# Seeding the third PSUM bank of a Strassen block with a ScalarE copy of the first product

## The chip, the cores and the metric

The kernel runs on one core of a Trainium2 chip. The metric is the device time of one execution in microseconds (us). The engines are TensorE (PE in the profile, with PEld for its weight loads), VectorE (DVE), ScalarE (ACT), GpSimd (POOL) and SyncE (SP). PSUM, into which TensorE writes, has eight banks; the kernel keeps four of them for long sums and four for everything short.

## The reference

Two decoder layers over 256 tokens of width 1024, all in float32. Each layer is a mixer (retention in layer 0, block attention in layer 1) between two RMS norms, and then an MLP with a squared ReLU, whose hidden width is 4096:

```python
def sq_relu_mlp(x, w_up, w_down):
    h = jax.nn.relu(x @ w_up)
    return (h * h) @ w_down
...
for i in range(DEPTH):
    pre, post, w_in, w_out, mpre, mpost, w_up, w_down = layers[i]
    h = h + rms_norm(mixers[i % N_MIXERS](rms_norm(h, pre), w_in, w_out), post)
    h = h + rms_norm(sq_relu_mlp(rms_norm(h, mpre), w_up, w_down), mpost)
```

The change touches the product `x @ w_up` alone.

## The kernel before

**Splitting.** A float32 product is made of three fast matmuls. Every weight tile (128 x 1024, a chunk) is split by `Stream.split`: ScalarE writes the rounded high part `whi` (line 175), VectorE the rest `wlo` (line 176). The function `mm` then issues high x high (line 232), high x low (line 233) and low x high (line 234). The activations are split in the same way (lines 251 and 252). Chunks are prepared ahead of their use, in ten pairs of buffers.

**The MLP.** The 256 tokens are two blocks of 128 (t = 0, 1), and the hidden width is eight groups of 512. Groups 0 and 1 are computed plainly. The other six are done two at a time by `up_blocks(g, down)`, for g = 2, 4, 6, so there are three such blocks in each layer's MLP and six in the kernel; in this text they are blocks 1 to 6, the first three in layer 0. A block computes a 2 x 2 product by seven products of half the depth (Strassen's scheme in Winograd's form) instead of eight. Each product is twelve matmuls of 512 columns. They collect in three PSUM banks `x`, `y`, `z` (px, py, pz in the profile), and between them stands `down()`, which does one step of the second matmul of the MLP, `(h*h) @ w_down`, over both token blocks (tile dn).

**Sums in a block.** The first product goes to x, is copied to SBUF by ScalarE (p1, line 518), and x goes on collecting. y collects without it, and so wherever y is needed VectorE adds p1 from SBUF: for u2 (line 527), for u3 (line 531), and for the last quarter (line 463, called with `add=p1`). The next product into y has to wait until u2 has been read from it, since it overwrites what u2 is.

**Squares.** `squared` applies ReLU and square on ScalarE (lines 466, 467), waits some planned time, turns the tile by four TensorE transposes into a bank `tp_u` (line 256), and splits that into the hidden activations (lines 251 and 252). These hidden tiles are the operands of later `down()` steps.

**The order.** The order of instructions is written out when the program is built: `Flow` keeps a planned clock that moves on with every matmul, chains such as `squared` yield delays in it, and each engine then runs its instructions strictly in that order. Only semaphores decide the real times.

**The banks.** `new_ps` takes one of the four short banks that is free by the written order; it may be written only once all readers of its last tenant are done. In the last MLP (layer 1) one of the four is taken by `dn4` for the whole of it:

```python
acc = [[new_acc("dn") for _ in range(2)] for _ in range(NT)]
if nxt is None:
    acc[1] = [acc[1][0], acc[1][1][:, :256], new_ps([P, 256], "dn4")]
```

Of the kernel before, what the change touches and what calls it, by code (L numbers as in the profile page):

```python
# [13 lines left out]
AF = mybir.ActivationFunctionType  # L14
# [3 lines left out]
P = 128  # L18
# [198 lines left out]
def body(ctx, tc, xT, x, gT, gpost, w_in_0, w_out_0, w_up_0, w_down_0, w_in_1, w_out_1, w_up_1, w_down_1,  # L217
         cs0, dT, cs1, cmask, out):
    nc = tc.nc
# [17 lines left out]
    def mm_rows(o, a, w, s, first, last, again=False):  # L237

        mm(o, a, (w.hi[:, s], w.lo[:, s]), first, last, again)
        n = s.stop - s.start  # L240
        ws.used(w, n * P)
        flow.advance()
# [7 lines left out]
    def split(hi, lo, src):  # L250
        nc.scalar.activation(hi, src, AF.Copy)  # L251
        nc.vector.tensor_sub(lo, src, hi.bitcast(F32))  # L252

    def turn4(tp, src):
        for j in range(4):
            nc.tensor.transpose(out=tp[:, j, :], in_=src[:, j * P:(j + 1) * P], identity=ident)  # L256
        flow.now += 4 * P / 1200

    def new_act():
        return act.tile([P, 2048], F32R, tag="act", name="act")  # L260

    def new_acc(name):
        return psa.tile([P, 512], F32, tag="acc", name=name)

    def new_ps(shape, name):
        return psb.tile(shape, F32, tag="ps", name=name)

    def new_e2(shape, name):
        return work.tile(shape, F32, tag="e2", name=name, bufs=6)
# [4 lines left out]
    def small_t(tag, n=1):  # L274
        return small.tile([P, n], F32, tag=tag, name=tag)
# [53 lines left out]
    def load_gain(i):  # L329
        gb = work.tile([P, D], F32, tag="gb", name="gb", bufs=1)  # L330
        nc.sync.dma_start(gb, gpost[i:i + 1, :].to_broadcast([P, D]))
        return gb
# [58 lines left out]
    def step_out(acc, lhs, k, t, w, nk):  # L391
        a = lhs(k, t)
        c0 = 0
        for o in acc[t]:
            n = o.shape[-1]
            mm_rows(o, a, w, slice(c0, c0 + n), k == 0, k == nk - 1)
            c0 += n
# [32 lines left out]
    def in_groups_skewed(hT, then, ready=None):  # L430

        held = []
        hT.ready(0)
        for g in range(2):
            held.append([])
            o = new_acc("ip")
            for c in range(4):
                held[g].append(ws.get())
                in_tile(hT, held[g][c], c, 0, o)
            then(g, 0, o)  # L440
        hT.ready(1)
        if ready:
            ready()
        for g in range(2):
            o = new_acc("ip")
            for c in range(4):
                in_tile(hT, held[g][c], c, 1, o)
            then(g, 1, o)


    def mlp(hT, gain, nxt, gi, qpool):
        ws.open_quads([qpool.tile([P, 2, CH], F32, name=f"quad{i}") for i in range(4)])
        hid = [None] * NG
        done = [[] for _ in range(NG)]

        def new_hid(g):
            hid[g] = new_act().rearrange("p (u j s) -> p u j s", u=2, j=4)

        def squared(g, t, o, add=None, sign=1.0, delay=4.0):

            c = new_e2([P, 512], "c")
            if add is not None:
                nc.vector.tensor_add(c, o, add)
                yield 2.2
                o = c
            nc.scalar.activation(c, o, AF.Relu, scale=sign)
            nc.scalar.activation(c, c, AF.Square)
            yield delay
            tp = new_ps([P, 4, P], "tp_u")
            turn4(tp, c)  # L470
            ts = slice(t * P, (t + 1) * P)
            split(hid[g][:, 0, :, ts], hid[g][:, 1, :, ts], tp)

        def square(g, *args):
            done[g].append(flow.spawn(squared(g, *args)))

        s_hi, s_lo = [p.tile([P, 4, 4, P], F32R, name=n, tag="act" if p is act else n)
                      for p, n in ((act, "s_hi"), (qpool, "s_lo"))]

        def block_sums():  # L480

            (a11, a12), (a21, a22) = [[hg[:, t, e::2, :] for e in range(2)] for t in range(NT)]
            f = [new_e2([P, 4, P], "hsum") for _ in range(4)]
            nc.vector.tensor_sub(f[0], a22, a21)
            yield 1.5
            nc.vector.scalar_tensor_tensor(f[1], f[0], -1.0, a11, op0=ALU.mult, op1=ALU.subtract)
            split(s_hi[:, 0], s_lo[:, 0], f[0])
            yield 2.8
            nc.vector.tensor_sub(f[2], a11, a21)
            split(s_hi[:, 1], s_lo[:, 1], f[1])  # L490
            yield 2.8
            nc.vector.scalar_tensor_tensor(f[3], f[1], -1.0, a12, op0=ALU.mult, op1=ALU.subtract)
            split(s_hi[:, 2], s_lo[:, 2], f[2])
            yield 2.8
            split(s_hi[:, 3], s_lo[:, 3], f[3])

        def quad(t, e):
            return lambda kp: hT.tile(2 * kp + e, t)

        def hsum(i):  # L500
            return lambda kp: (s_hi[:, i, kp, :], s_lo[:, i, kp, :])

        def product(o, lhsT, first):

            for half in range(2):
                w = ws.get()
                for kk in range(2):
                    kp = 2 * half + kk
                    mm_rows(o, lhsT(kp), w, slice(kk * 512, (kk + 1) * 512), first and kp == 0, kp == 3,
                            not first)  # L510

        def up_blocks(g, down):


            x = new_ps([P, 512], "px")
            product(x, quad(0, 0), True)
            p1 = new_e2([P, 512], "p1")
            nc.scalar.activation(p1, x, AF.Copy)
            down()
            flow.finish(*sums)  # L520
            z = new_ps([P, 512], "pz")
            product(z, hsum(0), True)
            down()
            y = new_ps([P, 512], "py")
            product(y, hsum(1), True)
            u2 = new_e2([P, 512], "u2")
            nc.vector.tensor_add(u2, y, p1)
            down()
            product(y, hsum(2), False)
            u3 = new_e2([P, 512], "u3")  # L530
            nc.vector.tensor_add(u3, y, p1)
            square(g + 1, 1, z, u3, -1.0, 6.0)
            down()
            product(x, quad(0, 1), False)
            square(g, 0, x, None, 1.0, 6.5)
            down()
            product(y, quad(1, 1), False)
            square(g, 1, y, p1)
            down()
            product(z, hsum(3), False)  # L540
            square(g + 1, 0, z, u2, -1.0)
            down()
            down()

        def lhs(k, t):
            g, j = divmod(k, 4)
            flow.finish(*done[g])
            return hid[g][:, 0, j, t * P:(t + 1) * P], hid[g][:, 1, j, t * P:(t + 1) * P]

        new_hid(0)  # L550
        new_hid(1)
        sums = []
        in_groups_skewed(hT, lambda g, t, o: square(g, t, o, None, 1.0, 3.6),
                         lambda: sums.append(flow.spawn(block_sums(), 1.0)))
        gb = load_gain(gain)
        rs2 = []
        for t in range(NT):
            r2 = small_t("rs2")
            nc.gpsimd.tensor_tensor(r2, hT.rs[t], hT.rs[t], ALU.mult)
            rs2.append(r2)  # L560
# [3 lines that stand above are left out]
        nk = FF // P  # L564
        ks = iter(range(nk - SKEW))

        def down():
            k, w = next(ks), ws.get()
            for t in range(NT):
                step_out(acc, lhs, k, t, w, nk)  # L570

        for g in range(2, NG, 2):
            new_hid(g + 1)
            new_hid(g)
            up_blocks(g, down)
        ws.quads = None
        if nxt is not None:
            nxt = nxt()
            finish_out(acc, lhs, nk - SKEW, nk, rs2, gb, nxt, gi)
            return nxt  # L580
        finish_last(acc, lhs, nk, rs2, gb)
# [34 lines left out]
    hT = HT()  # L616
# [207 lines left out]
    hT = HT()  # L824
# [4 lines left out]
    with tc.tile_pool(name="qpool0", bufs=1) as qpool:  # L829
        hT = mlp(hT, 1, HT, 2, qpool)  # L830
# [170 lines left out]
    hT = HT()  # L1001
# [102 lines left out]
```

## Time and profile before

| | us |
|---|---|
| median of 3 runs (674.85 to 675.34) | 675.29 |
| the profiled execution, its own time | 675.31 |
| its span, first to last instruction | 673.5 |
| busy: PE | 663.2 (98%) |
| busy: DVE | 495.1 (74%) |
| busy: ACT | 409.3 (61%) |
| busy: POOL | 103.5 (15%) |

The busy time of PE is the union of pipelined matmuls. What one matmul takes of PE's time is therefore read from the distance between the starts of neighbours, and a wait from a distance that is longer than the others. Times in the rows are counted from the start of the span, and a row's line number is that of the kernel shown above; a helper's line is shared by all its callers, and the tile names tell them apart.

### The profile page before, as it was taken

To read this page: it belongs to the slowest core of one execution; us is meant where nothing else is said; L and a number is where in the kernel's file an instruction comes from. 1 tells how busy PE (TensorE), PEld (TensorE's weight loads), DVE (VectorE), ACT (ScalarE), POOL (GpSimd) and SP (SyncE) were. 2 spreads that over 40 slices of the span, in tenths; PEclk is the share of its full clock that TensorE was granted. 3 is DMA by queue.
4 is the path that set the end of the run, shared out by engine and by line. 5 is a ranking of instruction groups with operands and counts; after the bars stand their busy time and mean duration, and the time that the engine had idled before them with its cause. 6 is when DMAs were issued, how large, how long until landed. Compare 5 with 4: busy or idle time off the path is not lost.

```text
span 673.5 us, 9114 instructions
## 1 busy us (share of the span) xinstructions
PE 663.2 (98%) x3371; PEld 559.3 (83%) x3371; DVE 495.1 (74%) x595; ACT 409.3 (61%) x575; POOL 103.5 (15%) x162
## 2 busy tenths in 40 slices
PE   8999999999999999999999999999999999999996
PEld 6888898988888888888888888888888888888885
DVE  5579675674547998878975876776669998788733
ACT  6555644544536777856774766766567668566731
POOL 0024120111000111101100161914001111011001
PEclk9999999999999999999999999999999999999999
DMA  7867655446629489696648557544284997956511
GB/s 278 319 207 250 204 188 198 163 157 211 205 87 384 112 263 332 153 377 159 187 144 264 173 176 228 168 148 157 76 361 97 307 300 167 375 129 188 176 44 62
DMA packets 38924, 137.61 MB, mean 204 GB/s; under 512 B 4576, under 2 KB 4832, under 8 KB 38880
## 3 DMA queue, kind: packets, MB, share of 16 engines
q1 hardware_dynamic: 35280, 124.44, 52.2%
q0 software_dynamic: 3456, 12.58, 10.6%
q8 instruction: 26, 0.43, 0.3%
q14 instruction: 18, 0.15, 0.1%
q10 hardware_dynamic: 144, 0.02, 0.0%
HBM read 123.39 MB, written 1.05 MB: 185 GB/s over the span
## 4 chain that ended last, share of the span: by engine, by line
PE 91%; DMA 3%; issue 2%; DVE 1%; ACT 1%; POOL 1%; SPq 0%; POOLq 0%; DVEq 0%; ACTq 0%
PE ip L232 9%; PE ip L233 9%; PE ip L234 9%; PE dn L234 8%; PE dn L232 8%; PE dn L233 8%; PE out L234 3%; PE out L232 3%; PE out L233 3%; DMA raw<-in_w_in 3%; PE py L232 3%; PE py L234 2%; PE py L233 2%; PE tp_u L256 2%; PE px L232 2%
## 5 line engine op out<-in xcount | busy, mean ns | idle before, releaser
L176 DVE TENSOR_TENSOR wlo<-raw,whi 128x1024 fp32r<-128x1024 f32 (+1 forms) x179 | 214.8, 1220 | 57.6 <-ACT whi L175 56.7
L175 ACT ACTIVATE whi<-raw 128x1024 fp32r<-128x1024 f32 (+1 forms) x179 | 180.6, 1037 | 24.6 <-PE out L234 10.9
L232 PE MATMUL ip<-whi,act 128*128 128x512 f32 x288 | 114.2, 396 | 0.4 <-DVE csr L708 0.4
L233 PE MATMUL ip<-wlo,act 128*128 128x512 f32 x288 | 112.4, 390 | 0.0
L234 PE MATMUL ip<-whi,act 128*128 128x512 f32 x288 | 112.4, 390 | 0.0
L176 DVE TENSOR_TENSOR wlo<-quad,whi 128x1024 fp32r<-128x1024 f32 x84 | 101.1, 1222 | 13.0 <-ACT whi L175 12.7
L232 PE MATMUL dn<-whi,act 128*128 128x512 f32 (+1 forms) x288 | 106.8, 371 | 0.0
L234 PE MATMUL dn<-whi,act 128*128 128x512 f32 (+1 forms) x288 | 105.7, 367 | 0.0
L233 PE MATMUL dn<-wlo,act 128*128 128x512 f32 (+1 forms) x288 | 105.3, 366 | 0.0
L175 ACT ACTIVATE whi<-quad 128x1024 fp32r<-128x1024 f32 x84 | 86.6, 1050 | 22.6 <-DMA quad<-quad 17.2
L234 PEld LDWEIGHTS ip<-whi,act 128*128 128x128 f32 x288 | 54.1, 188 | 11.6
L232 PEld LDWEIGHTS ip<-whi,act 128*128 128x128 f32 x288 | 54.2, 188 | 11.0 <-issue 0.8
L233 PEld LDWEIGHTS ip<-wlo,act 128*128 128x128 f32 x288 | 54.2, 188 | 10.1
L234 PEld LDWEIGHTS dn<-whi,act 128*128 128x128 f32 x288 | 54.2, 188 | 9.8 <-DVE act L252 0.9
L233 PEld LDWEIGHTS dn<-wlo,act 128*128 128x128 f32 x288 | 54.3, 188 | 9.1
L232 PEld LDWEIGHTS dn<-whi,act 128*128 128x128 f32 x288 | 54.2, 188 | 9.0
L185 POOL DMA_DIRECT2D quad<-quad x24 | 21.1, 881 | 190.4 <-DMA raw<-in_w_down 75.2
L232 PE MATMUL out<-whi,act 128*128 128x512 f32 x96 | 37.8, 394 | 0.0
L234 PE MATMUL out<-whi,act 128*128 128x512 f32 x96 | 37.4, 390 | 0.0
L251 ACT ACTIVATE act<-tp_u 128x512 fp32r<-128x512 f32 x32 | 19.1, 596 | 30.1 <-PE tp_u L256 30.1
L233 PE MATMUL out<-wlo,act 128*128 128x512 f32 x96 | 37.4, 389 | 0.0
L232 PE MATMUL qk<-act,whi 128*128 128x256 f32 x128 | 36.7, 287 | 0.5 <-ACT whi L175 0.5
(187 smaller groups left out, 1098.6 us busy)
## 6 DMA issues: line engine op xcount, KB each, us to landing
raw<-in_w_in SPq DMA_DIRECT2D x72, 512.0 KB, 4.4
raw<-in_w_down SPq DMA_DIRECT2D x64, 512.0 KB, 5.5
quad<-in_w_up SPq DMA_DIRECT2D x48, 512.0 KB, 7.6
raw<-in_w_out SPq DMA_DIRECT2D x24, 512.0 KB, 4.1
quad<-quad POOLq DMA_DIRECT2D x24, 512.0 KB, 5.9
raw<-in_w_up SPq DMA_DIRECT2D x16, 512.0 KB, 3.4
gb<-in_gpost SPq DMA_DIRECT2D x4, 512.0 KB, 6.3
h<-in_x SPq DMA_DIRECT2D x2, 512.0 KB, 6.7
```

The lines of the kernel that those rows point to most:

```text
L175: nc.scalar.activation(hi[:, c], raw[:, c], AF.Copy)
L176: nc.vector.tensor_sub(lo[:, c], raw[:, c], hi[:, c].bitcast(F32))
L185: nc.gpsimd.dma_start(o, a, accum_op=ALU.add)
L232: nc.tensor.matmul(o, a[0], b[0], start=first, stop=False, skip_group_check=again)
L233: nc.tensor.matmul(o, a[0], b[1], start=False, stop=False, skip_group_check=again)
L234: nc.tensor.matmul(o, a[1], b[0], start=False, stop=last, skip_group_check=again)
L251: nc.scalar.activation(hi, src, AF.Copy)
L256: nc.tensor.transpose(out=tp[:, j, :], in_=src[:, j * P:(j + 1) * P], identity=ident)
```

## The change

```diff
             x = new_ps([P, 512], "px")
             product(x, quad(0, 0), True)
-            p1 = new_e2([P, 512], "p1")
-            nc.scalar.activation(p1, x, AF.Copy)
             down()
             flow.finish(*sums)
+            y = new_ps([P, 512], "py")
+            nc.tensor.matmul(y, hT.tile(0, 0)[0], s_hi[:, 0].rearrange("p k s -> p (k s)"), start=True, stop=True)
+            nc.scalar.activation(y, x, AF.Copy)
             z = new_ps([P, 512], "pz")
             product(z, hsum(0), True)
             down()
-            y = new_ps([P, 512], "py")
-            product(y, hsum(1), True)
+            product(y, hsum(1), False)
             u2 = new_e2([P, 512], "u2")
-            nc.vector.tensor_add(u2, y, p1)
+            nc.scalar.activation(u2, y, AF.Copy)
             down()
             product(y, hsum(2), False)
             u3 = new_e2([P, 512], "u3")
-            nc.vector.tensor_add(u3, y, p1)
+            nc.scalar.activation(u3, y, AF.Copy)
             square(g + 1, 1, z, u3, -1.0, 6.0)
             down()
             product(x, quad(0, 1), False)
             square(g, 0, x, None, 1.0, 6.5)
             down()
             product(y, quad(1, 1), False)
-            square(g, 1, y, p1)
+            square(g, 1, y)
```

The bank y is taken before z now. One matmul (line 522 of the changed kernel) writes 512 columns into it, with values that nobody reads, so that the bank counts as written; ScalarE then overwrites it with the first product (line 523), and all products into y add to that. u2 and u3 become plain ScalarE copies of y (lines 529 and 533), and the ReLU of the last quarter reads y itself.

TensorE in block 4 (the first of layer 1), from the transposes of the last plain square to the first product into z. Before (numbers are buffers; what stands in brackets is the engine whose semaphore is waited for):

```order
L256 MATMUL tp_u_4996<-ident_100,c_4947 128x128 [waits PE_49,Activation_49]
...
L234 MATMUL dn4_4960<-whi_4881,act_4722 128x256
L232 MATMUL pz_5022<-whi_4900,s_hi_4720 128x512 [waits PE_49]
L233 MATMUL pz_5022<-wlo_4901,s_hi_4720 128x512
...
L232 MATMUL py_5066<-whi_4972,s_hi_4720 128x512 [waits DVE_49]
```

The same place in the changed kernel:

```order
L256 MATMUL tp_u_4991<-ident_100,c_4944 128x128 [waits PE_49,Activation_49]
...
L234 MATMUL dn4_4957<-whi_4878,act_4719 128x256
L522 MATMUL py_5017<-s_hi_4717,act_4468 128x512 [waits PE_49]
L232 MATMUL pz_5020<-whi_4897,s_hi_4717 128x512 [waits DVE_49]
L233 MATMUL pz_5020<-wlo_4898,s_hi_4717 128x512
...
L232 MATMUL py_5017<-whi_4969,s_hi_4717 128x512 [waits Activation_49]
```

The wait for VectorE has moved from the first product into y to the first product into z, 21 matmuls of 512 columns and 6 of 256 earlier; in the built programs the bank of tp_u goes to py before the change and to pz after it.

VectorE in block 4 up to the read of that tp_u, in the changed kernel; before the change the same instructions stand there in the same order, only with other numbers:

```order
L252 TENSOR_TENSOR act_4719<-tp_u_4925,act_4719 128x4x128 [waits Activation_49]
L176 TENSOR_TENSOR wlo_4939<-raw_4742,whi_4938 128x1024 [waits DMAHW1_49,Activation_49]
L252 TENSOR_TENSOR s_lo_4718<-hsum_4845,s_hi_4717 128x512 [waits Activation_49]
L176 TENSOR_TENSOR wlo_4970<-quad0_4713,whi_4969 128x1024 [waits Activation_49]
L176 TENSOR_TENSOR wlo_4981<-quad0_4713,whi_4980 128x1024 [waits Activation_49]
L252 TENSOR_TENSOR act_4720<-tp_u_4991,act_4720 128x4x128 [waits Activation_49]
```

Nothing has moved here: the read of tp_u stays behind five others.

ScalarE in block 1, around the new copies u2 and u3, in the changed kernel:

```order
L175 ACTIVATE whi_2378<-quad3_2031 128x1024
L529 ACTIVATE u2_2388<-py_2328 128x512
L175 ACTIVATE whi_2393<-raw_2197 128x1024
L175 ACTIVATE whi_2405<-quad0_2028 128x1024
L175 ACTIVATE whi_2418<-quad0_2028 128x1024
L533 ACTIVATE u3_2428<-py_2328 128x512
L175 ACTIVATE whi_2435<-raw_2257 128x1024
```

Before the change the five splits (line 175) stand there without the two copies; the copies now stand between splits that are prepared for later products.

## Rows read from the trace of the kernel before

**Rows 1.** The page: span, engine busy times, granted TensorE clock in 40 slices.

```profile
span 673.5 us, 9114 instructions
PE 663.2 (98%) x3371; PEld 559.3 (83%) x3371; DVE 495.1 (74%) x595; ACT 409.3 (61%) x575; POOL 103.5 (15%) x162
...
PEclk9999999999999999999999999999999999999999
```

**Rows 2.** Waits of PE: who waited for whom, total us, times, longest us.

```profile
PE warm L283 <- DVE junk L278: 1.2, 1, 1.2
...
PE qk L234 <- DVE wlo L176: 0.4, 2, 0.2
```

**Rows 3.** Timeline of PE in block 1, product into z and its successor: start us, us.

```profile
236.55 0.39 PE L232 MATMUL pz<-whi,s_hi 128*128 128x512 f32 x1
...
239.28 0.39 PE L232 MATMUL dn<-whi,act 128*128 128x512 f32 x1
```

**Rows 4.** Timeline of PE in block 1, at the second product into y.

```profile
247.21 0.39 PE L234 MATMUL dn<-whi,act 128*128 128x512 f32 x1
247.62 0.47 PE L232 MATMUL py<-whi,s_hi 128*128 128x512 f32 x1
247.93 0.40 PE L233 MATMUL py<-wlo,s_hi 128*128 128x512 f32 x1
```

**Rows 5.** Timeline of PE in block 4, at the second product into y.

```profile
531.70 0.28 PE L234 MATMUL dn<-whi,act 128*128 128x256 f32 x1
531.88 0.47 PE L232 MATMUL py<-whi,s_hi 128*128 128x512 f32 x1
532.19 0.39 PE L233 MATMUL py<-wlo,s_hi 128*128 128x512 f32 x1
```

**Rows 6.** The tile py, columns: duration ns minimum/median/maximum, first and last start us.

```profile
L527 DVE TENSOR_TENSOR u<-py,p x6: 690/692/692, 246.8 to 615.7; 128x512 f32<-128x512 f32 x6
```

**Rows 7.** The tile px: same columns.

```profile
L518 ACT ACTIVATE p<-px x6: 577/580/582, 236.7 to 605.3; 128x512 f32<-128x512 f32 x6
```

**Rows 8.** Timeline of DVE in block 1 at the same place.

```profile
246.78 0.69 DVE L527 TENSOR_TENSOR u<-py,p 128x512 f32<-128x512 f32 x1
```

**Rows 9.** Timeline of ACT in block 1, around the place of u2; idle before, releaser.

```profile
241.47 1.99 ACT L175 ACTIVATE whi<-quad 128x1024 fp32r<-128x1024 f32 x2
243.37 1.04 ACT L175 ACTIVATE whi<-raw 128x1024 fp32r<-128x1024 f32 x1
246.10 1.06 ACT L175 ACTIVATE whi<-quad 128x1024 fp32r<-128x1024 f32 x1 [1.68 <-DMA quad<-quad]
```

**Rows 10.** Timeline in block 1: the last matmul of the first product into y.

```profile
244.49 0.39 PE L234 MATMUL py<-whi,s_lo 128*128 128x512 f32 x1
```

**Rows 11.** Timeline in block 1: the split behind u3 on DVE, its use on PE.

```profile
253.50 1.22 DVE L176 TENSOR_TENSOR wlo<-raw,whi 128x1024 fp32r<-128x1024 f32 x1
262.05 0.39 PE L233 MATMUL dn<-wlo,act 128*128 128x512 f32 x1
```

**Rows 12.** Timeline of DVE in block 1: the read of tp_u.

```profile
239.38 0.69 DVE L252 TENSOR_TENSOR act<-tp_u,act 128x512 fp32r<-128x512 f32 x1
```

**Rows 13.** Timeline of PE in block 4, from the transposes to the product into z.

```profile
518.70 0.60 PE L256 MATMUL tp_u<-ident,c 128*128 128x128 f32 x4
...
520.82 0.39 PE L232 MATMUL pz<-whi,s_hi 128*128 128x512 f32 x1
```

**Rows 14.** Timeline of DVE in block 4, at the same time.

```profile
519.03 0.69 DVE L252 TENSOR_TENSOR act<-tp_u,act 128x512 fp32r<-128x512 f32 x1
...
521.37 2.36 DVE L176 TENSOR_TENSOR wlo<-quad,whi 128x1024 fp32r<-128x1024 f32 x2
523.64 0.69 DVE L252 TENSOR_TENSOR act<-tp_u,act 128x512 fp32r<-128x512 f32 x1
```

**Rows 15.** Timeline in block 5: DVE's read of tp_u, PE's product into z.

```profile
563.35 0.69 DVE L252 TENSOR_TENSOR act<-tp_u,act 128x512 fp32r<-128x512 f32 x1
564.12 0.40 PE L232 MATMUL pz<-whi,s_hi 128*128 128x512 f32 x1
```

## The prediction

> **What bounds the kernel now.** I read the page's busy line first, then the waits of PE, then PE's timeline in the six blocks. PE is busy for 663.2 of 673.5 us and its granted clock is in the top tenth in all 40 slices, that is, 2.4 GHz [rows 1]. A high busy share alone would not say that PE sets the end, but the waits do: PE's list has five lines, the longest single wait is 1.2 us, at the start, and none of the five is in an MLP [rows 2]. In a block, the twelve 512-column matmuls of a product take 2.73 us from the first start to the start of what follows, 0.2275 each [rows 3]. So whatever is added to PE in a block is paid in full, and work taken from DVE (74%) or given to ACT (61%) [rows 1] moves the time only where PE waits for it. The question is therefore not what VectorE saves, but which waits of PE go and which come.
>
> **What the change adds to PE.** Six matmuls of 512 columns, one a block, in a stream that has no holes: 6 x 0.2275 = 1.37 us [rows 3]. From below this could be nothing for one that stands ahead of a wait; from above I take 0.31, the distance that a matmul right after a wait shows [rows 4, 5], so 6 x 0.31 = 1.86. I take 0.2275, since the matmul has the shape and type of its neighbours. The Trainium skill ("TensorE: Matmul & The Clock Gate", section "Back-to-back issue gap") puts a sustained stream of 512-column matmuls at about 131 ns each. This trace does not agree; by that figure, as an estimate, the six would be 0.79 us and the sum below 0.58 lower.
>
> **What it moves between ScalarE and VectorE.** VectorE loses three additions a block, 18 x 0.69 = 12.4 us [rows 6]. ScalarE keeps one copy (px into PSUM instead of SBUF) and gains two, 12 x 0.58 = 7.0 us [rows 7]. No row shows ScalarE writing PSUM: I take the 0.58 of the copy into SBUF, and even twice that ends long before the next product into y, which stands behind a product into z and a down step, 24 matmuls or 5.4 us [rows 3]. None of this is on PE's path by itself. Two effects are.
>
> First, a gain. The second product into y waits until u2 is read. In block 1 VectorE, which has a queue, reads it only at 246.78 to 247.47 [rows 8], and PE starts at 247.62: 0.41 after its neighbour instead of 0.23, and the matmul after it again 0.08 late, 0.27 in all [rows 4]. In block 4 it is 0.18 instead of the half of 0.23 for a 256-column neighbour, and again 0.08: 0.14 [rows 5]. The other four blocks show no such gap. On ScalarE, u2 stands behind two splits that end at 243.46 [rows 9], and y is ready at 244.88 [rows 10]: the copy ends near 245.7, some 1.5 us ahead of the old end, and before PE asks. So both gaps go: -0.41 us. The bound on the other side is that they stay: 0.
>
> Second, who is queued behind the two copies on ScalarE: splits of weights. The copies wait for PE there, so the split behind u2 starts some 2 us later than its 243.37 [rows 9]. That costs only if a weight comes late. The split behind u3 is finished by VectorE at 254.72 and used by PE at 262.05, 7.3 us later [rows 11]; VectorE, which does the second half of each split, has 0.69 less to do ahead of it. I cost this at nothing; it is paid from a delay of about 7 us on.
>
> The square of the last y quarter now skips one addition, so its transposes come some 2 us earlier on PE. There are as many as before, and ScalarE's ReLU and square have four planned us: nothing.
>
> **The bank.** This is the largest term, and the diff does not show it. y is taken before z, so at the start of the product into z four tiles must have a bank: x, y, z, and the last tp_u if it is still unread. In layer 0 there are four short banks, and it fits: in block 1 tp_u is read by VectorE only at 239.38, long after z began at 236.55, and nothing waits [rows 3, 12]. In layer 1 dn4 holds one of the four. In block 4 the tp_u of the last plain square is written at 518.70 and z begins at 520.82 [rows 13]; VectorE reads tp_u at 523.64 to 524.33, because two splits of 2.36 us together stand before it in its queue [rows 14]. Before the change y took that bank, one product and one down step later, and it was free by then. In the changed program y takes the last free bank and z takes that of tp_u, so the first matmul into z waits for VectorE, and the whole of PE behind it, in order. VectorE's queue up to there is the same as before and runs without gaps, so its end stays at 524.33. PE starts 0.15 us after such a release (247.47 to 247.62) [rows 4, 8], at 524.48, and would have been ready at 520.82 + 0.23 = 521.05: 3.43 us, and 0.08 for the matmul after the wait. Together 3.51 us. Nothing gives this back: behind it PE has no long waits in layer 1's MLP that could absorb it [rows 2].
>
> Blocks 5 and 6 have the same three banks. There VectorE's read ended at 564.04 and z began at 564.12 [rows 15]; the new z comes 0.23 later and waits for 0.15 after the read, so it would be on time by 0.16 even unchanged. VectorE has additions less ahead of it, so I cost this at nothing; as an upper bound, 0.3 us a block if the read slips.
>
> **The sum.** 675.31 (the profiled execution; its span is 673.5, and 1.8 lies around it) + 1.37 + 3.51 - 0.41 = 679.78. The profiled execution is 0.02 above the median 675.29, so no correction: **679.8 us**, 0.7% slower. Its own range: down to 678.9 (the wait 0.5 shorter, the matmul of block 4 and one more at nothing), up to 680.9 (+0.5 for matmuls at 0.31, +0.6 for blocks 5 and 6).
>
> **Rivals.**
>
> *The bank is free in time* (not slower). If VectorE's read of tp_u ended before about 520.9 in block 4, z would not wait, and the time is 675.31 + 1.37 - 0.41 = 676.3, within 0.2% of the median (that is, up to 676.6), which is about what a measurement of this kernel can tell from no change. For it: in the other five blocks the bank is in time. Against it: it needs 3.4 us on VectorE, whose order there has not moved and whose removed additions all come later. Chance 0.10.
>
> *The clock falls.* A gap of 3.4 us on PE is three times the longest in this trace [rows 2], and all stretches of it have 2.4 GHz [rows 1]; what PE does after so long a gap is not shown. If it went on at 1.2 GHz for the product into z, twelve matmuls would cost 12 x 0.2275 = 2.7 us more, 682.5. Against it: the 1.2 us gap at the start left no mark. The Trainium skill (same page, section "HAM oscillation — how this bites in real kernels") says that waits of TensorE can put its clock back to half. No row here shows it. Chance 0.10.
>
> *ScalarE's waits starve PE of weights.* From a delay of 7 us [rows 11], which would take several of the new waits in a row with the waits for DMA that stand there already (1.68 us at 246.10 [rows 9]). Priced at 2 us or more, 681.8 and up. Chance 0.03.
>
> *VectorE's relief pays more than the six matmuls cost.* This would have to come from waits of PE that I don't see. Chance 0.01.
>
> **How the numbers follow.** The forecast has 0.76, the free bank 0.10, the clock 0.10, starved weights 0.03, relief 0.01. The range is the forecast's own with the clock case, 678.9 to 682.5, which holds 0.86. Slower by over 0.2%: 0.76 + 0.10 + 0.03 = 0.89; the same: 0.10; faster: 0.01.
>
> **What would show it.** In the new trace: the extra matmul of each block 0.23 before the next start; a hole of some 3.4 us in PE in block 4 alone, at the first matmul into z, released by VectorE's read of tp_u (line 252); no gap at the second product into y in blocks 1 and 4; u2 and u3 on ScalarE near 0.58; blocks 2, 3, 5 and 6 longer by 0.23 each. No hole in block 4 makes the forecast wrong at its largest term; a hole with a granted clock below 9 tenths behind it is the clock rival.

## The result and the profile after

The changed kernel takes 681.07 us (median of 6 runs, 680.76 to 682.2), the kernel before on the same chip 675.4 (674.85 to 676.2): ratio 1.0082, 95% interval 1.0072 to 1.0093. It is slower by 5.7 us. The profiled execution took 681.0 us, its span is 679.2.

The page of the changed kernel, in the form of [rows 1]:

```profile
span 679.2 us, 9111 instructions
...
PE 666.3 (98%) x3377; PEld 561.6 (83%) x3377; DVE 485.0 (71%) x577; ACT 414.5 (61%) x587; POOL 105.6 (16%) x162
...
PEclk9999999999999999999999999999999999999999
```

VectorE's busy time fell by 10 us and ScalarE's rose by 5, and neither shows in the time. PE's busy time grew by 3.1 us for six matmuls of 0.23, which come to 1.4 only; the clock line, in tenths of a slice of 17 us, gives no reason. Both are answered only from nearer.

The waits of PE, as in [rows 2] (total us, times, longest):

```profile
PE pz L232 <- DVE act L252: 3.2, 1, 3.2
...
PE warm L283 <- DVE junk L278: 1.2, 1, 1.2
```

One line is new, and it is the longest: the first matmul of a product into z waits once for VectorE's splitting of tp_u. PE's timeline in block 4 (start us, us; in brackets idle before and releaser) shows it at the place of [rows 13]:

```profile
520.83 0.39 PE L522 MATMUL py<-s_hi,act 128*128 128x512 f32 x1
524.38 0.50 PE L232 MATMUL pz<-whi,s_hi 128*128 128x512 f32 x1 [3.17 <-DVE act L252]
524.73 0.40 PE L233 MATMUL pz<-wlo,s_hi 128*128 128x512 f32 x1
...
525.67 0.39 PE L234 MATMUL pz<-whi,s_lo 128*128 128x512 f32 x1
525.89 0.58 PE L232 MATMUL pz<-whi,s_hi 128*128 128x512 f32 x1
526.27 0.63 PE L233 MATMUL pz<-wlo,s_hi 128*128 128x512 f32 x1
...
529.26 0.44 PE L234 MATMUL dn<-whi,act 128*128 128x512 f32 x1
529.54 0.39 PE L232 MATMUL dn<-whi,act 128*128 128x512 f32 x1
```

From 520.83 to 524.38 are 3.55 us for one matmul of 0.23: a hole of 3.32, and the matmul behind it comes another 0.12 late. The next five run at the usual distance. From 525.89 on, the distance is mostly 0.43 instead of 0.23, up to 529.54: nine matmuls take 3.65 us, where 9 x 0.2275 = 2.05 would do. That is 1.60 us lost where PE is busy and waits for nothing. VectorE's timeline has the releaser at the same time as in [rows 14]:

```profile
523.65 0.68 DVE L252 TENSOR_TENSOR act<-tp_u,act 128x512 fp32r<-128x512 f32 x1
```

It ends at 524.33, and PE starts 0.05 later. The windows of the same stretch (window, length, busy us of PE, PEld, DVE, ACT, POOL with instructions, granted clock, DMA share, GB/s) name what made the nine matmuls slow:

```profile
520.83:524.38 3.55, 0.39 (x3) 0.07 (x1) 3.55 (x6) 3.55 (x6) 1.16 (x2) 1.00 0.72 265
524.38:526.27 1.89, 1.89 (x7) 1.52 (x8) 1.89 (x2) 1.89 (x3) 0.58 (x1) 0.91 1.12 247
526.27:529.50 3.23, 3.23 (x9) 2.57 (x8) 3.23 (x4) 1.48 (x2) 0.00 (x0) 0.52 1.00 192
529.50:534.00 4.50, 4.50 (x24) 3.79 (x23) 1.64 (x2) 0.00 (x0) 0.00 (x0) 1.00 1.04 317
```

The granted clock is 0.52 from 526.27 to 529.50, that is 1.2 GHz for nearly all of it, and 2.4 GHz again behind it. PE had stood idle for 3.3 us shortly before. The Trainium skill ("TensorE: Matmul & The Clock Gate", section "HAM oscillation — how this bites in real kernels") says that waits of TensorE can send its clock back to half; this trace agrees, with 0.52 behind the hole of 3.3 us.

How much of the 5.7 us is in this one place is read from the first matmul into x, at which a block starts. Block 4 of the changed kernel begins and ends at:

```profile
514.61 0.40 PE L232 MATMUL px<-whi,act 128*128 128x512 f32 x1
...
563.30 0.40 PE L232 MATMUL px<-whi,act 128*128 128x512 f32 x1
```

That is 48.69 us, where it was 43.52 before (514.60 to 558.12). The table gives four blocks of each kernel that is spoken of here, each from its first matmul into x to that of the next block, and the stretch from the start of block 1 to the start of the kernel's last matmul. This stretch leaves out the first 230 us, whose length differs by more than 1 us between profiles. The clock has a part in that too. In four of the twelve profiles here (changed with 4 in the hole; changed, y behind z; before, no dn4; changed, no seeding matmul) the granted clock is 0.50 from 10 to 12 us after the start, and block 1 starts at 231.31 to 231.63; in the eight others it stays at 1.00 there, and block 1 starts at 229.94 to 230.88. One of the four, with y behind z, has in the window from 10 to 20 us:

```profile
10.00:20.00 10.00, 10.00 (x75) 10.00 (x75) 8.42 (x12) 7.15 (x11) 0.00 (x0) 0.86 0.87 310
```

The kernel's first 230 us are the same work in all twelve. PE's longest wait between its first matmul and that stretch is 0.7 to 1.0 us in the four, and 0.2 to 1.4 in the others.

| kernel | block 1 | block 2 | block 4 | block 5 | block 1 to last matmul | less before |
|---|---|---|---|---|---|---|
| before | 43.33 | 42.73 | 43.52 | 43.18 | 436.60 | |
| changed | 43.22 | 42.96 | 48.69 | 43.42 | 442.54 | +5.94 |
| changed, 14 matmuls in the hole | 43.23 | 42.96 | 47.08 | 43.41 | 440.94 | +4.34 |
| changed, 4 in the hole | 43.21 | 42.96 | 47.07 | 43.41 | 440.92 | +4.32 |
| changed, 8 in the hole | 43.23 | 42.96 | 47.10 | 43.41 | 440.97 | +4.37 |
| before, bank taken in block 4 | 43.31 | 42.73 | 49.71 | 43.17 | 442.73 | +6.13 |
| changed, y behind z | 43.24 | 42.96 | 44.58 | 43.42 | 438.48 | +1.88 |
| before, no dn4 | 43.31 | 42.74 | 43.30 | 42.74 | 434.99 | -1.61 |
| changed, no dn4 | 43.24 | 42.96 | 43.27 | 42.97 | 435.82 | -0.78 |
| before, four more matmuls a block | 43.92 | 43.63 | 44.29 | 44.08 | 441.55 | +4.95 |
| changed, copies on VectorE | 43.26 | 42.96 | 49.76 | 43.42 | 443.68 | +7.08 |
| changed, no seeding matmul | 43.01 | 42.73 | 43.39 | 43.19 | 436.13 | -0.47 |

In the changed kernel blocks 2 and 5 are longer by 0.23 and 0.24, the one matmul each. Block 1 is shorter by 0.11: 0.23 more for the matmul, and some 0.3 less, since the gap of [rows 4] is gone:

```profile
247.13 0.39 PE L234 MATMUL dn<-whi,act 128*128 128x512 f32 x1
247.36 0.39 PE L232 MATMUL py<-whi,s_hi 128*128 128x512 f32 x1
247.59 0.39 PE L233 MATMUL py<-wlo,s_hi 128*128 128x512 f32 x1
```

Block 4 is longer by 5.17: 0.23 for the matmul, 3.32 for the hole, 0.12 behind it, 1.60 at the slow clock, less the 0.14 of [rows 5], together 5.13.

### The profile page after: what moved, and what is told of

The parts are those of the page before. It is cut to its first block, busy times and chain, and to the rows that moved or that the text cites. A ratio compares the mean times of both kernels' runs of the same rounds, so it can differ in the third digit from the quotient of the medians.

```text
span 679.2 us, 9111 instructions
## 1 busy us (share of the span) xinstructions
PE 666.3 (98%) x3377; PEld 561.6 (83%) x3377; DVE 485.0 (71%) x577; ACT 414.5 (61%) x587; POOL 105.6 (16%) x162
## 4 chain that ended last, share of the span: by engine, by line
PE 91%; DVE 2%; issue 2%; ACT 2%; DMA 1%; POOL 1%; POOLq 0%; DVEq 0%; SPq 0%; ACTq 0%
PE ip L232 9%; PE ip L234 9%; PE ip L233 9%; PE dn L234 8%; PE dn L232 8%; PE dn L233 8%; PE out L234 3%; PE out L232 3%; PE out L233 3%; PE py L232 2%; PE py L233 2%; PE py L234 2%; PE tp_u L256 2%; PE qk L234 2%; PE qk L232 2%
## 5 line engine op out<-in xcount | busy, mean ns | idle before, releaser
L234 PE MATMUL qk<-act,wlo 128*128 128x256 f32 x128 | 36.4, 285 | 0.4 <-DVE wlo L176 0.4
```

The lines of the kernel that those rows point to most:

```text
L234: nc.tensor.matmul(o, a[1], b[0], start=False, stop=last, skip_group_check=again)
```

## The experiments

The theory after the result: the loss is the bank that z has to wait for in block 4, plus the slow clock that follows from PE's idleness there. The rivals are that the slow stretch has another cause than the hole, that the wait comes from the new order of instructions and not from a missing bank, and that ScalarE's new copies cost part of it.

### The hole and the clock

If the slow clock comes from the hole, it should go once PE has something to do in it. In block 4 of the changed kernel, matmuls that nobody reads follow the seeding one:

```diff
             nc.tensor.matmul(y, hT.tile(0, 0)[0], s_hi[:, 0].rearrange("p k s -> p (k s)"), start=True, stop=True)
+            if nxt is None and g == 2:
+                for _ in range(14):
+                    nc.tensor.matmul(y, hT.tile(0, 0)[0], s_hi[:, 0].rearrange("p k s -> p (k s)"), start=True, stop=True)
             nc.scalar.activation(y, x, AF.Copy)
```

> The changed kernel with 14 more unread matmuls into y behind the seeding matmul, in block 4 alone: 15 x 0.2275 = 3.4 us, about as long as TensorE's wait for the bank there. Theory (the wait lasts until VectorE has read tp_u, and the slow matmuls behind it come from the idle gap, through the granted clock): the product into z starts as late as without them, no gap is left, the granted clock stays at its upper level, the twelve matmuls take 2.75 us instead of 4.03, and the time falls by 1.6 to 1.7 us, to about 679.4. Rival (the slow matmuls come from what else runs at that moment, ScalarE writing PSUM or the transfers): they stay at 0.43 us apart, and the time stays at 681.1. Second rival (the wait is counted from the seeding matmul's end): the time rises to some 684.

Measured: 680.72 us, ratio 1.0072 (1.0057 to 1.0087). PE's timeline at the end of the fill:

```profile
523.65 1.07 PE L525 MATMUL py<-s_hi,act 128*128 128x512 f32 x4
524.69 0.50 PE L232 MATMUL pz<-whi,s_hi 128*128 128x512 f32 x1
525.03 0.39 PE L233 MATMUL pz<-wlo,s_hi 128*128 128x512 f32 x1
```

The product into z starts no earlier, since VectorE's read still releases it, and yet block 4 lasts 47.08 us instead of 48.69: 1.61 less, with fourteen matmuls more. The granted clock is 1.00 from 521.36 to 530.00. So the 1.6 us were the clock's, and work without a use in the hole takes them away. The median over four executions misses the expected 679.4: it is 4.9 us above the kernel before, where the changed kernel is 5.7 above it, so 0.8 less instead of 1.6. The profiled execution took 679.69 at a mean granted clock of 0.999, the three others 680.48 to 681.47 at 0.994 to 0.998; where the clock fell in those isn't kept. So the 1.6 us rest on the blocks of the profile.

How much of the hole has to be filled was asked with the same edit and four and eight matmuls.

> The changed kernel, with four more unread matmuls into y behind the seeding matmul of block 4: 4 x 0.2275 = 0.91 us of the hole is filled, so PE should stand for about 3.3 - 0.9 = 2.4 us, and z starts no earlier than before (VectorE's read releases it). Theory (the slow clock follows from the hole that is left): the smaller hole either still brings the clock to 1.2 GHz, block 4 then lasts 48.7 to 49.8 us as without the fill, or it does not, block 4 then lasts 47.1 as with 14 matmuls; anything between would say that the slow stretch gets shorter with the hole. Rival (the slow stretch comes from the matmul into a bank that ScalarE writes, not from the hole): block 4 near 48.7 whatever the fill; but that was already against the run with 14.

> The changed kernel, with eight more unread matmuls into y behind the seeding matmul of block 4: 8 x 0.2275 = 1.82 us of the hole is filled, so PE should stand for about 3.3 - 1.8 = 1.5 us. Theory: as with four; the 1.2 us wait at the kernel's start and the 0.8 us hole of the run with y behind z left the clock at 2.4 GHz, so I expect no slow stretch here: block 4 lasts 47.1 us. Rival: the clock falls at any hole over 1 us: block 4 48.7 or more.

Measured in one execution each: 680.66 and 679.93 us. With four, PE's timeline reads:

```profile
522.39 1.09 PE L525 MATMUL py<-s_hi,act 128*128 128x512 f32 x4
525.70 0.50 PE L232 MATMUL pz<-whi,s_hi 128*128 128x512 f32 x1 [2.22 <-DVE act L252]
526.04 0.39 PE L233 MATMUL pz<-wlo,s_hi 128*128 128x512 f32 x1
```

And the window behind the hole, with the columns from above:

```profile
525.70:531.00 5.30, 5.30 (x25) 4.45 (x26) 5.30 (x5) 3.38 (x4) 0.59 (x1) 1.00 1.06 236
```

The hole is 2.40 us (525.70 less 522.39 and 4 x 0.2275). With eight it is 1.50 (524.94 less 521.62 and 8 x 0.2275):

```profile
521.62 1.97 PE L525 MATMUL py<-s_hi,act 128*128 128x512 f32 x8
524.94 0.50 PE L232 MATMUL pz<-whi,s_hi 128*128 128x512 f32 x1 [1.34 <-DVE act L252]
525.28 0.40 PE L233 MATMUL pz<-wlo,s_hi 128*128 128x512 f32 x1
```

Neither shows a slow stretch in block 4, which lasts 47.07 and 47.10: the same as with the hole filled. So here holes of 1.5 and 2.4 us left the clock alone, and one of 3.3 did not. As each is one profile, the runs don't say whether a hole of 2.4 us does so each time; and at the start of the kernel the clock fell behind waits of at most 1.0 us in four profiles, and not behind one of 1.4, so the length of the hole is not all that decides.

### The bank, without the change

If the missing bank is the cause, taking it away from the kernel before should be enough. This kernel is that of before, but with y taken ahead of z in every block, and in block 4 alone written there, by one unread matmul; nothing is seeded, and VectorE's additions stay:

```diff
+            y = new_ps([P, 512], "py")
+            if nxt is None and g == 2:
+                nc.tensor.matmul(y, hT.tile(0, 0)[0], s_hi[:, 0].rearrange("p k s -> p (k s)"), start=True, stop=True)
             z = new_ps([P, 512], "pz")
             product(z, hsum(0), True)
             down()
-            y = new_ps([P, 512], "py")
             product(y, hsum(1), True)
```

> The kernel before with one unread matmul into y ahead of the product into z, in block 4 alone; nothing is seeded, VectorE adds p1 as before. Theory (y taking a bank before z is the cause): one matmul of 0.23 us makes z wait 3.3 us for tp_u's bank and brings the clock down behind it: 675.4 + 0.23 + 3.3 + 1.7 - 0.14 (the gap at u2 in block 4 is covered) = 680.5. Rival (the loss needs the seeding, ScalarE's copies or the moved additions): 675.6.

Measured: 682.21 us, ratio 1.009 (1.0071 to 1.011). PE's timeline in block 4, and then the windows of the hole and of what follows:

```profile
521.30 0.39 PE L523 MATMUL py<-s_hi,act 128*128 128x512 f32 x1
524.85 0.79 PE L232 MATMUL pz<-whi,s_hi 128*128 128x512 f32 x1 [3.16 <-DVE act L252]
525.45 0.63 PE L233 MATMUL pz<-wlo,s_hi 128*128 128x512 f32 x1
```

```profile
521.30:524.85 3.55, 0.39 (x3) 0.07 (x1) 3.55 (x6) 3.55 (x6) 1.16 (x2) 0.85 0.70 249
524.85:530.14 5.29, 5.29 (x13) 4.13 (x13) 5.29 (x5) 3.45 (x4) 0.58 (x1) 0.50 1.06 228
```

The same hole, with the same releaser, from a single matmul and a bank taken earlier: block 4 is longer by 6.19 us, and blocks 1, 2 and 5 not at all. The order of the other work, the seeding and ScalarE's copies are not needed for the loss. What differs is the clock: here it fell while PE still stood (0.85 over the hole), the whole product into z ran at 1.2 GHz, and block 4 is 49.71 - 47.08 = 2.6 us above the filled one, instead of 1.6. The 680.5 that were expected, with 1.7 for the clock, fall short of the measured time, in part by this.

### The bank given back

The other way round: both kernels with four short banks in layer 1 too. The edit to each is the same:

```diff
-        if nxt is None:
-            acc[1] = [acc[1][0], acc[1][1][:, :256], new_ps([P, 256], "dn4")]
```

The kernel before with it:

> The kernel before, without the lines that give dn4 one of the four short banks in layer 1: four short banks in both layers; the last sum is then one bank of 512 columns instead of two of 256. It is the base for the same edit of the changed kernel. Expected by both theories: within 0.5% of the kernel before (the end of the kernel may gain or lose a little, since the last output comes in one piece), blocks 4, 5 and 6 as long as before within 0.3 us.

The changed kernel with it:

> The changed kernel, without the lines that give dn4 one of the four short banks in layer 1. Theory (the loss is a missing bank in block 4, and what the clock makes of the hole): y, z and the last tp_u have a bank each, there is no wait at the first product into z, no slow clock behind it, and the difference from the kernel before with the same edit is the six matmuls less the vanished gaps, 1.37 - 0.41 = +1.0 us (+0.14%); block 4 lasts about 43.6 us instead of 48.7. Rival (the loss comes from the order of the work or from ScalarE's copies, not from the bank): a wait of about 3 us stays in block 4, and the difference stays near +5.7 us (+0.8%).

Measured: 674.75 us (10 runs), ratio to the kernel before 0.9985 (0.9976 to 0.9994), and 674.98 us (10 runs), 0.9987 (0.9978 to 0.9996). The change costs 0.2 us between them by the medians, and 0.83 from block 1 to the last matmul. In the changed one, PE's and VectorE's timelines in block 4 read:

```profile
521.57 0.39 PE L522 MATMUL py<-s_hi,act 128*128 128x512 f32 x1
521.79 0.39 PE L232 MATMUL pz<-whi,s_hi 128*128 128x512 f32 x1
...
524.40 0.68 DVE L252 TENSOR_TENSOR act<-tp_u,act 128x512 fp32r<-128x512 f32 x1
```

VectorE reads tp_u as late as ever, and z starts 2.6 us ahead of that read. Block 4 lasts 43.27 us, as long as block 1. So the wait was for a bank and for nothing else, and with it the slow clock goes. The expected difference was +1.0 us; 0.83 is near it, and the times of whole executions can't tell 0.2 from 1.0.

These two kernels are also the only ones here that are clearly faster than the kernel before, by 0.15% and 0.13%. The gain has nothing to do with the seeding, since the one without it has it too: it is in layer 1's MLP (before, blocks 4 and 5 are shorter by 0.22 and 0.44, blocks 1 and 2 by 0.02 at most), where one matmul of 512 columns takes the place of two of 256, 96 fewer by the page. That this is the cause fits, but no run isolates it.

### The bank, one product later

In between lies a third order, with the seeding kept: y is taken behind the product into z, one down step earlier than in the kernel before, and z gets the free bank again.

```diff
-            y = new_ps([P, 512], "py")
-            nc.tensor.matmul(y, hT.tile(0, 0)[0], s_hi[:, 0].rearrange("p k s -> p (k s)"), start=True, stop=True)
-            nc.scalar.activation(y, x, AF.Copy)
             z = new_ps([P, 512], "pz")
             product(z, hsum(0), True)
+            y = new_ps([P, 512], "py")
+            nc.tensor.matmul(y, hT.tile(0, 0)[0], s_hi[:, 0].rearrange("p k s -> p (k s)"), start=True, stop=True)
+            nc.scalar.activation(y, x, AF.Copy)
             down()
```

> The changed kernel with the seeding matmul and ScalarE's copy into y moved behind the product into z, so that z takes the last free bank in block 4 and y that of tp_u, as before the change. Theory (bank): the product into z no longer waits; the seeding matmul waits instead from the end of z, near 523.6, to VectorE's read of tp_u at 524.33, that is 0.8 us, with no fall of the clock: 675.4 + 1.37 (six matmuls) + 0.8 + 0.1 - 0.4 (gaps at u2 gone) = 677.3. Rival (the loss in block 4 comes from the seeding itself, the matmul or ScalarE writing PSUM, wherever it stands): about 681.

Measured: 677.46 us (9 runs), ratio 1.0028 (1.0018 to 1.0038). PE's timeline in block 4:

```profile
524.97 0.39 PE L234 MATMUL pz<-whi,s_lo 128*128 128x512 f32 x1
526.01 0.50 PE L524 MATMUL py<-s_hi,act 128*128 128x512 f32 x1 [0.66 <-DVE act L252]
526.35 0.39 PE L232 MATMUL dn<-whi,act 128*128 128x512 f32 x1
```

The same wait for the same bank, but shorter by the product that now stands ahead of it: a hole of 0.81 us (526.01 - 524.97 - 0.23), and the distances behind it are 0.34 once and then 0.23 again. Block 4 is longer by 1.06 than before. Two thirds of the loss are gone, and what stays is the six matmuls and 0.9 us of wait.

### The price of a matmul

Four unread matmuls go into z ahead of each product into z of the kernel before, so 24 in all; no bank is taken earlier.

```diff
             z = new_ps([P, 512], "pz")
+            for _ in range(4):
+                nc.tensor.matmul(z, hT.tile(0, 0)[0], s_hi[:, 0].rearrange("p k s -> p (k s)"), start=True, stop=True)
             product(z, hsum(0), True)
```

> The kernel before with four unread matmuls into z ahead of each of the six products into z, 24 in all, in z's own bank, which is free then. Theory (TensorE is the bound and each costs its distance): 24 x 0.2275 = 5.46, less the 0.41 of gaps at u2, which VectorE now meets: 675.4 + 5.05 = 680.4, and six such matmuls cost 1.37. Rival (they hide in part under waits or run at a higher rate): under 679, or 678.1 at 0.131 us each.

Measured: 681.63 us (4 runs), ratio 1.0092 (1.0076 to 1.0109). Block 2 runs between these two rows of PE's timeline:

```profile
273.87 0.39 PE L232 MATMUL px<-whi,act 128*128 128x512 f32 x1
...
317.50 0.39 PE L232 MATMUL px<-whi,act 128*128 128x512 f32 x1
```

43.63 us against 42.73 before: 0.90 for four, 0.225 each, and block 5 gives the same. Such a matmul is paid in full. Blocks 1 and 4 grew by 0.59 and 0.77 only, that is, their gaps at the second product into y went without any change of ScalarE or VectorE, since PE asks later. From block 1 to the last matmul it is +4.95; the ratio's interval, from 5.1 us up, lies a little above that. The profiled execution is the fastest of the four (679.87, mean granted clock 0.999); the others took 681.43 to 682.81 at 0.992 to 0.996. So the excess goes with a lower clock, but as they have no trace, where it fell is not shown.

### The move from VectorE to ScalarE

The two copies of a block go to VectorE, and the rest of the change stays:

```diff
-            nc.scalar.activation(u2, y, AF.Copy)
+            nc.vector.tensor_copy(u2, y)
...
-            nc.scalar.activation(u3, y, AF.Copy)
+            nc.vector.tensor_copy(u3, y)
```

> The changed kernel, with the copies u2 and u3 on VectorE instead of ScalarE; the bank's seeding stays. Theory: the wait at the product into z in block 4 and the slow clock behind it stay (block 4 about 48.7 us), and the gap at the second product into y comes back in block 1 (about 0.27 us), since VectorE reads u2 late again: 0 to 0.4 us above the changed kernel, about 681.3. Rival (ScalarE's two copies a block hold up splits and are a part of the loss): at least 0.5 us below the changed kernel, 680.5 or less.

Measured: 682.55 us (4 runs), ratio 1.0103 (1.0089 to 1.0116). Blocks 1, 2 and 5 are within 0.04 us of the changed kernel's, so ScalarE's copies hold up nothing, and that rival falls. The theory missed too, twice. The gap in block 1 did not come back: VectorE's and PE's timelines read

```profile
246.38 0.68 DVE L529 COPY u<-py 128x512 f32<-128x512 f32 x1
...
247.25 0.40 PE L232 MATMUL py<-whi,s_hi 128*128 128x512 f32 x1
```

VectorE reads u2 as late as before: 16.44 us after the start of block 1 (246.38 - 229.94; in [rows 8] 246.78 - 230.34), and is done at 247.06. But PE comes later, since the seeding matmul stands ahead of it: the product starts 17.31 us after the start of the block (247.25 - 229.94), no earlier than the 17.28 to which it had to wait before (247.62 - 230.34). So the one matmul more is hidden in the old gap, as in the kernel with 24. And block 4 is longer by 1.07 than in the changed kernel. The windows from the hole on say where:

```profile
520.50:524.35 3.85, 0.69 (x6) 0.37 (x5) 3.85 (x6) 3.85 (x6) 1.17 (x2) 0.87 0.61 227
524.35:526.27 1.92, 1.92 (x5) 1.53 (x6) 1.92 (x2) 1.92 (x3) 0.58 (x1) 0.50 1.13 271
526.27:529.50 3.23, 3.23 (x9) 2.55 (x8) 3.23 (x4) 1.55 (x2) 0.00 (x0) 0.50 1.02 204
```

The instructions up to z and the hole are those of the changed kernel; the clock is not. It fell in the hole (0.87), as in the kernel with only the bank taken, and block 4 is 49.76 - 47.08 = 2.7 us above the filled one. So the same hole cost 1.6 to 2.7 us of clock, by where in it or behind it the clock fell. Each figure is from one execution; whether the kernel or the execution sets that place, the runs don't show.

### What the seeding would be worth without its matmul

The last kernel leaves out the matmul that opens the bank and takes y behind z. By the Trainium skill ("PSUM — Partial Sum Buffer", section "The four PSUM rules"), a write by ScalarE does not mark a bank as written, and a matmul that follows overwrites what is not marked; in this kernel the first product can therefore be lost from y, in whole or in part, and its time is that of the schedule alone. No row of a trace here shows those marks.

```diff
-            y = new_ps([P, 512], "py")
-            nc.tensor.matmul(y, hT.tile(0, 0)[0], s_hi[:, 0].rearrange("p k s -> p (k s)"), start=True, stop=True)
-            nc.scalar.activation(y, x, AF.Copy)
             z = new_ps([P, 512], "pz")
             product(z, hsum(0), True)
+            y = new_ps([P, 512], "py")
+            nc.scalar.activation(y, x, AF.Copy)
             down()
```

> The changed kernel, with the seeding matmul left out and y taken behind the product into z: ScalarE's copy alone writes the first product into the bank, and all products into y add to it. Theory: no PE work is added and PE waits for no bank (in block 4 it is ScalarE's copy that waits for VectorE's read of tp_u, and PE needs y only after the down step that follows), so the time is that of the kernel before less the two gaps at the second product into y: 675.3 - 0.4 = 674.9, ratio 0.9994; block 1 lasts 43.0 and block 4 43.4 us. Rival 1: ScalarE, standing at the bank in block 4, comes late with the splits of weights or with the copy, and PE waits for it: over 676.5. Rival 2: the moved additions (VectorE's relief) are worth more than the two gaps: below 674.2.

Measured: 675.5 us (11 runs), ratio 0.9997 (0.9988 to 1.0006). Block 1 lasts 43.01 us and block 4 43.39, 0.32 and 0.13 less than before: the two gaps of [rows 4, 5], and hardly anything else. The expected ratio, 0.9994, lies inside the interval. In block 4 the timelines of VectorE, ScalarE and PE read

```profile
524.24 0.69 DVE L252 TENSOR_TENSOR act<-tp_u,act 128x512 fp32r<-128x512 f32 x1
524.97 0.58 ACT L524 ACTIVATE py<-px 128x512 f32<-128x512 f32 x1
...
526.92 0.40 PE L232 MATMUL py<-whi,s_hi 128*128 128x512 f32 x1
```

The copy comes right behind VectorE's read of tp_u and is done 1.4 us before PE needs it, so neither rival shows. That is the whole profit there was to be had from moving 18 additions, 12.4 us by their durations, off VectorE: 0.5 us from block 1 to the last matmul, less than the times of whole executions tell from nothing.

## Why the prediction was right, and by how much not

The forecast was 679.8, and the profiled execution took 681.0: slower, for the reason given, 1.2 us above the forecast. It is inside the range of 678.9 to 682.5, but above the 680.9 at which the forecast's own range ended (whose lower end its terms put at 678.8); only the clock rival took the range further. By the sign that the prediction itself named, a granted clock below 9 tenths behind the hole, that rival is what came, on top of the bank, with 1.60 us instead of its 2.7. That the sum came so near is the bank's doing; that the time fell inside the range is owed to a rival held unlikely.

- **The bank** (forecast 3.51, measured 3.32 + 0.12 = 3.44). The place, the releaser and the end of VectorE's read (524.33) came as the rows said. PE started 0.05 after it instead of the 0.15 of [rows 4, 8], and the matmul behind came 0.12 late instead of 0.08. Taking the bank alone makes the same hole, and giving it back removes it.
- **The six matmuls** (1.37). 0.23 and 0.24 in blocks 2 and 5, and 0.225 in the kernel with 24. The 131 ns of the Trainium skill ("TensorE: Matmul & The Clock Gate", section "Back-to-back issue gap") do not hold here.
- **The two gaps** (-0.41). They are gone, and a little more in block 1. The reason was half of it: ScalarE's earlier copy is enough (the kernel without the seeding matmul shows it), but so is PE coming later by itself (the kernels with 24 matmuls and with the copies on VectorE).
- **ScalarE and VectorE** (nothing). The copy into PSUM, which no row showed, has the same length as the one into SBUF of [rows 7]. From the tile py of the changed kernel (ns minimum/median/maximum):

```profile
L523 ACT ACTIVATE py<-px x6: 576/578/586, 238.8 to 613.5; 128x512 f32<-128x512 f32 x6
L529 ACT ACTIVATE u<-py x6: 598/598/600, 244.8 to 621.4; 128x512 f32<-128x512 f32 x6
```

- **Blocks 5 and 6** (nothing). Neither waits. In block 5, the timelines of VectorE and PE that answer to [rows 15] have z on time, by 0.6 us:

```profile
568.23 0.68 DVE L252 TENSOR_TENSOR act<-tp_u,act 128x512 fp32r<-128x512 f32 x1
...
569.53 0.40 PE L232 MATMUL pz<-whi,s_hi 128*128 128x512 f32 x1
```

- **The clock** (nothing in the forecast; a rival of its own with 2.7). This is the step that failed: it was given a chance of 0.10 and no place in the sum, with the wait of 1.2 us at the start as evidence against it. That row could not carry this. It spoke of a wait a third as long as the forecast one, and one that lies ahead of the kernel's first matmul; in block 4 holes of 0.8, 1.5 and 2.4 us left the clock alone as well, while that of 3.3 did not, in three profiles of three. And it was one profile: in four of the twelve the same start, with waits no longer than these, did bring the clock to 0.50. As a price, 2.7 was the upper end of what the runs showed (1.6 in the changed kernel's profile, 2.6 and 2.7 in two others).

The sum with measured terms: 1.37 + 3.44 - 0.41 + 1.60 = 6.00, beside 5.94 from block 1 to the last matmul. The first 230 us were 0.28 us shorter in the profile of the changed kernel (block 1 starts at 230.06 instead of 230.34), which leaves 5.72, beside the 5.69 between the two profiled executions.

## What to carry to other kernels

A tile that is taken earlier costs a bank for longer: before moving an allocation, count the banks that are still unread at that moment, in every phase of the kernel, and look up who reads the last one and how late that engine is. A hole in TensorE's stream that is longer than any in the trace is not priced by its length alone; time behind it at half the clock has to be weighed in the sum, and one profile in which a shorter wait left no mark is no evidence against it. Work taken off an engine is worth only the waits that the bound engine has for it: here 12.4 us of VectorE were worth 0.5 us. And times in two traces are compared from a common event, such as the start of a block, not from the start of the span.

## What the runs showed of the hardware that was not expected

- A hole of 3.3 us in TensorE's stream was followed by 3.65 us (525.89 to 529.54) mostly at a distance of 0.43 us between matmuls of 512 columns, instead of 0.23, though the first six matmuls behind it came at 0.35 once and then at 0.23. In two other profiles, with a hole of the same length, the clock fell within the hole and no matmul of the product into z was fast. All three profiles with this hole show a slow stretch in block 4; holes of 0.8, 1.5 and 2.4 us there, one profile each, show none.
- At the start of the kernel the clock fell to 0.50 in four of twelve profiles, for some 3 to 4 us, with waits of at most 1.2 us before it, and stayed at 1.00 in eight with the same work; the four have neither the longest nor the shortest waits. So one execution does not show what the clock does in the next.
- Matmuls that nobody reads kept the clock up: with 4, 8 and 14 of them in the hole it stayed at 1.00 in block 4 (one profile each), and four, 0.9 us of work, made that block shorter by 1.6 us.
- One matmul of 0.23 us, put where it takes a bank, made a block longer by 6.2 us.
